# A two-layer YOCO decoder trunk on one core: a second weight unit in the four quarters of the first loads

## The chip, the core and the metric

The kernel runs on one NeuronCore of a Trainium2 chip. The core has five engines with instruction queues of their own: TensorE (PE; PEld is its weight load), VectorE (DVE), ScalarE (ACT), GpSimd (POOL) and SyncE (SP), which here only issues transfers. Each queue is worked off strictly in the order in which it was written; an instruction that has to wait holds up everything behind it on its engine. The metric is the device time of one execution in microseconds (us), lower is better. The kernel before took 583.97 us (median of 3 runs, 583.82 to 584.67).

## The reference

One sequence of 256 tokens with 1024 features passes two layers and a final norm:

```
x = x + short_conv_mixer(rms_norm(x, a_norm), a_w_in, a_conv, a_w_out)     # layer 0
x = x + conv_glu_ffn(rms_norm(x, f_norm[0]), ...)
k, v = shared_kv(x, kv_norm, w_k, w_v)                                     # layer 1
x = x + moba_attention(rms_norm(x, b_norm), w_q, w_o, k, v, rel_bias)
x = x + conv_glu_ffn(rms_norm(x, f_norm[1]), ...)
return rms_norm(x, final_norm)

def rms_norm(x, g):  return x * rsqrt(mean(x * x, axis=-1) + 1e-6) * g
def short_conv_mixer(h, w_in, conv_w, w_out):
    b_gate, c_gate, hx = split(h @ w_in, 3)
    return (b_gate * causal_dwconv(c_gate * hx, conv_w)) @ w_out
```

All is float32. The change lies in the first layer's mixer, in the first 30 us or so.

## The kernel before

**Products.** x is held transposed, as `xT`: 8 tiles of 128 features by 256 tokens. Every float32 product is made of three products of rounded halves (`mm3`, L160): both operands are split into a `hi` part (a copy to a shorter format, by ScalarE, L86) and a `lo` part (what is left, a subtraction by VectorE, L92). TensorE multiplies hi by hi (L161), hi by the input's lo (L162) and the weight's lo by hi (L163). So the third matmul on a weight is the first that needs its `lo`. The norm's factor 1/rms is not applied to x: x is only scaled by the gain (`scaled_hi`, `scaled_lo`), and the products are multiplied by `rr`, the row of factors, when they are read.

**Units.** Weights come in units: "B" of 1 MB (128 x 2048) and "S" of 512 KB (128 x 1024). A unit is loaded by SP (`load`), split (`split_hi`, `split_lo`, also in parts) and then used by matmuls (`up_step`, `down_step`). `hi("B")` and `lo("B")` split the next unit of a kind by counters (`ptr`); a finished `lo` also issues the load of the unit three further on, into the same raw buffer. The mixer has 8 steps: `MC[j]` (B) gives the c gate and the hx part, `MB[j]` (S) the b gate, `MO[j]` (S) is its piece of the output product. A B unit is 48 matmuls, an S unit 24.

**The start.** L134 runs ten float32 matmuls on a tile of ones. `pk`, the table of gains and conv weights, is loaded from ScalarE's queue behind ScalarE's table load. SP loads x, `MC[0]` and `MB[0]` in four quarters (two feature tiles each), then `MC[1]` in four quarters, then whole units. The first loop (L375) takes a quarter of x, `MC[0]` and `MB[0]` at a time. A second loop (L385) splits `MC[1]` in quarters and takes the squares of x (ScalarE), which VectorE sums.

**The factors.** `rstd_cols` (L316) sums the squares over the features with two small matmuls (L320), VectorE makes 1/rms out of it in eleven small steps and two of a diagonal `dg` (L328). `rstd_rows` (L331) turns `dg` into a row with a matmul (L334), which ScalarE copies into `rr`. `mixer_a` (L397) multiplies the products of `MC[j]` by `rr` (L401, L402), and then has in VectorE's queue the `lo` of another unit, the conv taps (L369) and more. `mixer_b` (L413) multiplies by the b gate and splits the result for `MO[j]`. In the order of the program `rstd_cols` stands after six of eight feature tiles of `MC[1]`, `rstd_rows` after two of eight of `MC[2]`. `MB[2]` writes to the bank named `misc`, which `rstd_cols` and `rstd_rows` use as well.

The order on every engine is the order in which the program issues instructions; no scheduler changes it. DMA transfers rotate through eight completion semaphores, so a transfer is issued only when the eighth before it has landed.

Of the kernel before, what the change touches and what calls it, by code (L numbers as in the profile page):

```python
# [32 lines left out]
P_AN, P_KVN, P_BN, P_FN, P_FIN, P_CONV, P_FCW, P_FCB = 0, 8, 16, 24, 40, 48, 72, 336  # L33
# [4 lines left out]
def f32(ap):  # L38
    return ap.bitcast(F32)
# [3 lines left out]
def yoco_kernel(ctx: ExitStack, tc: tile.TileContext, t: dict, out: bass.AP):  # L43
    nc = tc.nc
    V, A, G, PE = nc.vector, nc.scalar, nc.gpsimd, nc.tensor

    const = ctx.enter_context(tc.tile_pool(name="const", bufs=1))
# [12 lines left out]
    ptr = {"B": [0, 0], "S": [0, 0]}  # L60
# [36 lines left out]
    def hi(tag, part=0, parts=1):  # L97

        n = ptr[tag][0]
        if n < len(by_tag[tag]) and (by_tag[tag][n].prev is None or by_tag[tag][n].prev.used):  # L100
            by_tag[tag][n].split_hi(part, parts)
            ptr[tag][0] += part == parts - 1

    def lo(tag, part=0, parts=1):

        n = ptr[tag][1]
        if n < len(by_tag[tag]) and by_tag[tag][n].hi is not None:
            by_tag[tag][n].split_lo(part, parts)
            if part == parts - 1:
                ptr[tag][1] += 1  # L110
                if n + RAW_BUFS[tag] < len(by_tag[tag]):
                    by_tag[tag][n + RAW_BUFS[tag]].load()

    MC = [Unit(t["w_mc"][j], BIG) for j in range(KT)]
    MB, MO = [], []
# [15 lines left out]
    ones = const.tile([128, 128], F32, name="ones")  # L131
    G.memset(ones, 1.0)
    warm = psum.tile([128, 512], F32, name="misc", bufs=1)
    for _ in range(10):  # L134
        PE.matmul(warm[:, :128], ones, ones, start=True, stop=True)
    first = const.tile([128, 1], F32, name="first")
    A.activation(first, ones[:, 0:1], AF.Copy)
    xT = act.tile([128, KT, S], F32, name="xres", bufs=1)
    pk = const.tile([128, P_ALL], F32, name="pk")
    nc.scalar.dma_start(pk[:, :P_FCW], t["pk"][:, :P_FCW])  # L140
    for q in range(4):
        nc.sync.dma_start(xT[:, 2 * q:2 * q + 2, :], t["xT"][:, 2 * q:2 * q + 2, :])
# [13 lines left out]
    def par(c, k=0):  # L156
        return pk[:, c + k:c + k + 1]
# [7 lines left out]
    def up_step(u, o, xh, xl, m, ks=range(KT), first=0, again=False):  # L165

        assert u.lo is not None
        wh, wl = u.v(u.hi, m), u.v(u.lo, m)
        for k in ks:
            h, lw = (xh.again, xl.again) if again and k == 0 else (xh[:, k, :], xl[:, k, :])  # L170
            for i in range(m):
                mm3(o[:, i, :], wh[:, k, i, :], wl[:, k, i, :], h, lw,
                    start=(k == first and i == 0), stop=(k == KT - 1))
        u.used = ks[-1] == KT - 1
# [49 lines left out]
    def acc_bank():  # L224
        return psum.tile([128, 2, S], F32, name="acc", bufs=4)

    def up_bank():
        return psum.tile([128, 2, S], F32, name="up", bufs=3)
# [27 lines left out]
    def parts_tiles(moved=False):  # L256
        return Rows("xh", moved), Rows("xl", moved)
# [17 lines left out]
    def sum_squares(sq, half, order=same):

        f = 4 * half
        V.tensor_add(sq[:, f:f + 2, :], sq[:, f:f + 2, :], sq[:, f + 2:f + 4, :])
        if half:
            V.tensor_add(sq[:, 0:2, :], sq[:, 0:2, :], sq[:, 4:6, :])  # L280
            V.tensor_add(sq[:, 2, :], order(sq[:, 0, :]), order(sq[:, 1, :]))

    def square_tile():
        return act.tile([128, KT, S], F32, name="sq", tag="oh", bufs=1)
# [31 lines left out]
    def rstd_cols(sq):  # L316

        ps = psum.tile([128, 512], F32, name="misc", bufs=1)
        for c in range(2):
            PE.matmul(ps[:, c:c + 1], sq[:, 2, c * 128:(c + 1) * 128], ones[:, 0:1],  # L320
                      start=(c == 0), stop=True, skip_group_check=True)
        w = tmp.tile([128, 8], F32, name="nw")
        ms, y, a = w[:, 0:2], w[:, 2:4], w[:, 4:6]
        V.tensor_scalar(ms, ps[:, 0:2], 1.0 / D, EPS, op0=OP.mult, op1=OP.add)
        rsqrt(ms, y, a)
        dg = tmp.tile([128, 2, 128], F32, name="dg", tag="bias")
        for c in range(2):
            V.tensor_scalar(dg[:, c, :], ident, y[:, c:c + 1], None, op0=OP.mult)  # L328
        return y, dg
# [41 lines left out]

    mc, mb, z = {}, {}, {}
    xh, xl = parts_tiles()
    mc[0], mb[0] = up_bank(), acc_bank()
    for q in range(4):  # L375
        scaled_hi(xT, P_AN, (2 * q, 2 * q + 1), xh)
        scaled_lo(xT, P_AN, (2 * q, 2 * q + 1), xh, xl)
        hi("B", q, 4)
        lo("B", q, 4)
        hi("S", q, 4)  # L380
        lo("S", q, 4)
        up_step(MC[0], mc[0], xh, xl, 2, (2 * q, 2 * q + 1))
        up_step(MB[0], mb[0], xh, xl, 1, (2 * q, 2 * q + 1))
    sq = square_tile()
    for q in range(4):  # L385
        hi("B", q, 4)
        squares(xT, sq, q)
        lo("B", q, 4)
        if q == 2:
            sum_squares(sq, 0)  # L390
    sum_squares(sq, 1)
    tile_0_again(xh, xl)
    hi("S")
# [25 lines left out]
            lo(fill)  # L419
        zl()  # L420

    mc[1] = acc_bank()
    up_step(MC[1], mc[1], xh, xl, 2, range(1, 7), first=1)
    _, dg = rstd_cols(sq)
    for q in range(4):
        hi("B", q, 4)
        lo("B", q, 4)
    hi("S")
    hi("B")
    up_step(MC[1], mc[1], xh, xl, 2, (0, 7), first=1, again=True)  # L430
    mb[1] = acc_bank()
    up_step(MB[1], mb[1], xh, xl, 1)
    mc[2] = up_bank()
    up_step(MC[2], mc[2], xh, xl, 2, range(0, 2))
    rr = rstd_rows(dg)
    A.activation(rr[:, 1, :], rr[:, 0, :], AF.Square)
    lo("S")
    up_step(MC[2], mc[2], xh, xl, 2, range(2, 8))
    mb[2] = psum.tile([128, 512], F32, name="misc", bufs=1).rearrange("p (a s) -> p a s", s=S)
    up_step(MB[2], mb[2], xh, xl, 1)  # L440
    for i in range(2):
# [34 lines left out]
    xh, xl, sq = boundary(acc, xT, P_FN)  # L476
# [85 lines left out]
    xvh, xvl, sq = boundary(acc, xT, P_KVN, rev)  # L562
# [157 lines left out]
    for kind, n in heads:  # L720
        if kind == "v":
            vb[n] = acc_bank() if n < 3 else up_bank()
            if n == 1:
                v_step(1, range(0, 4))
                bias_table(hot)
                ycol, dg = rstd_cols(sq)
# [58 lines left out]
    xh, xl, sq = boundary(acc, xT, P_FN + KT, moved=True)  # L785
# [131 lines left out]
```

## Time and profile before

| | |
|---|---|
| median of 3 runs | 583.97 us |
| the profiled execution | 584.08 us, span 582.1 us |
| TensorE busy | 573.4 us, 98% of the span |
| VectorE busy | 460.9 us, 79% |
| ScalarE busy | 359.7 us, 62% |
| chain that ended last | TensorE 97%, DMA 1%, ScalarE 1% |
| moved | 108.51 MB, 186 GB/s on average |

The span is the time from the first to the last instruction of the program, and lies within the execution's time. Busy shares are averages over the whole program; the chain that ended last is followed back from the last instruction to what released it each time, so its shares say what set the end. With TensorE at 98%, what remains is where it isn't busy, and that is in the first 10 us and at the end.

### The profile page before, as it was taken

How to read it: one execution, taken by the hardware profiler on the slowest of the kernel's cores; microseconds unless marked ns; L12 is line 12 of the kernel's file. 1: busy time of each engine (PE TensorE's matmuls, PEld its weight loads, DVE VectorE, ACT ScalarE, POOL GpSimd, SP SyncE). 2: the span in 40 equal slices, each digit the busy share in tenths (PEclk: the TensorE clock that was granted, in tenths of full speed). 3: DMA queues.
4: the chain of work that ended last, by engine and by line, in shares of the span. 5: the costliest groups of instructions: out<-in, count | busy, mean ns of one | idle time of the engine just before them, and what ended most of it. 6: DMA issues, size and time to landing. Idle time of an engine off the chain costs nothing.

```text
span 582.1 us, 11537 instructions
## 1 busy us (share of the span) xinstructions
PE 573.4 (98%) x4745; PEld 558.4 (96%) x4745; DVE 460.9 (79%) x781; ACT 359.7 (62%) x570; POOL 3.6 (1%) x15
## 2 busy tenths in 40 slices
PE   8999999999999999999999999999999999999995
PEld 8999999999999999999999999999999999999994
DVE  5899769888778777877977887757997787777865
ACT  7765347566566555665758997748675566556443
POOL 0000000000000000000000000000000000000001
PEclk9999999999999999999999999999999999999999
DMA  8985673545554566544446564434655644553111
GB/s 290 404 285 195 214 256 114 212 147 217 217 187 166 191 217 213 173 167 175 147 171 220 181 243 165 145 110 146 218 180 218 216 169 169 207 216 117 65 37 73
DMA packets 24236, 108.51 MB, mean 186 GB/s; under 512 B 2759, under 2 KB 5496, under 8 KB 16248
## 3 DMA queue, kind: packets, MB, share of 16 engines
q1 hardware_dynamic: 23864, 107.46, 52.1%
q8 instruction: 37, 0.61, 0.4%
q10 hardware_dynamic: 320, 0.32, 0.2%
q14 instruction: 15, 0.12, 0.1%
HBM read 106.70 MB, written 1.07 MB: 185 GB/s over the span
## 4 chain that ended last, share of the span: by engine, by line
PE 97%; DMA 1%; ACT 1%; DVE 0%; issue 0%; SPq 0%; POOLq 0%; POOL 0%; DVEq 0%; ACTq 0%
PE up L161 20%; PE up L163 20%; PE up L162 20%; PE acc L161 7%; PE acc L163 7%; PE acc L162 6%; PE acc L189 3%; PE acc L188 3%; PE acc L187 3%; PE acc L623 1%; PE acc L579 1%; PE acc L581 1%; PE acc L582 1%; DMA xres<-xT 1%; PE up L582 0%; PE up L579 0%
## 5 line engine op out<-in xcount | busy, mean ns | idle before, releaser
L161 PE MATMUL up<-xh,hiB 128*128 128x256 f32 x944 | 263.2, 279 | 0.3 <-ACT hiB L86 0.3
L163 PE MATMUL up<-xh,loB 128*128 128x256 f32 x944 | 261.5, 277 | 0.2 <-DVE loB L92 0.2
L162 PE MATMUL up<-xl,hiB 128*128 128x256 f32 x944 | 261.7, 277 | 0.0
L161 PEld LDWEIGHTS up<-xh,hiB 128*128 128x128 f32 x944 | 177.5, 188 | 1.6 <-ACT hiB L86 0.6
L162 PEld LDWEIGHTS up<-xl,hiB 128*128 128x128 f32 x944 | 177.5, 188 | 0.8
L163 PEld LDWEIGHTS up<-xh,loB 128*128 128x128 f32 x944 | 177.4, 188 | 0.7 <-DVE loB L92 0.7
L92 DVE TENSOR_TENSOR loB<-rawB,hiB 128x2048 fp32r<-128x2048 f32 (+2 forms) x75 | 147.6, 1973 | 3.9 <-ACT hiB L86 3.9
L86 ACT ACTIVATE hiB<-rawB 128x2048 fp32r<-128x2048 f32 (+1 forms) x73 | 123.6, 1697 | 17.2 <-PE acc L582 6.0
L92 DVE TENSOR_TENSOR loS<-rawS,hiS 128x1024 fp32r<-128x1024 f32 (+2 forms) x73 | 83.7, 1148 | 13.8 <-ACT hiS L86 13.5
L498 ACT ACTIVATE cv<-u,pk 128x256 f32<-128x256 f32 x88 | 48.2, 595 | 72.8 <-DVE u L491 72.8
L369 DVE SCALAR_TENSOR_TENSOR cv<-u,pk,cv 128x255 f32<-128x255 f32 x192 | 81.4, 479 | 2.7 <-ACT cv L498 1.7
L86 ACT ACTIVATE hiS<-rawS 128x1024 fp32r<-128x1024 f32 (+1 forms) x71 | 71.6, 1010 | 9.7 <-PE acc L162 6.0
L491 DVE TENSOR_TENSOR u<-up,rr 128x512 f32<-128x512 f32 x44 | 30.3, 689 | 58.7 <-PE up L163 57.3
L161 PE MATMUL acc<-sh,hiS 128*128 128x256 f32 x240 | 66.3, 276 | 0.0
L163 PE MATMUL acc<-sh,loS 128*128 128x256 f32 x240 | 66.3, 276 | 0.0
L162 PE MATMUL acc<-sl,hiS 128*128 128x256 f32 x240 | 66.3, 276 | 0.0
L366 ACT ACTIVATE sh<-hid 128x256 fp32r<-128x256 f32 x52 | 21.7, 416 | 59.7 <-DVE hid L512 55.0
L163 PEld LDWEIGHTS acc<-sh,loS 128*128 128x128 f32 x240 | 45.1, 188 | 0.0
L161 PEld LDWEIGHTS acc<-sh,hiS 128*128 128x128 f32 x240 | 45.1, 188 | 0.0
L162 PEld LDWEIGHTS acc<-sl,hiS 128*128 128x128 f32 x240 | 45.1, 188 | 0.0
L189 PE MATMUL acc<-hiS,sl 128*128 128x512 f32 (+1 forms) x89 | 34.8, 391 | 0.0
L188 PE MATMUL acc<-loS,sh 128*128 128x512 f32 (+1 forms) x89 | 34.6, 389 | 0.0
(157 smaller groups left out, 756.9 us busy)
## 6 DMA issues: line engine op xcount, KB each, us to landing
rawB<-w_up SPq DMA_DIRECT2D x44, 1024.0 KB, 4.8
rawS<-w_dn SPq DMA_DIRECT2D x44, 512.0 KB, 3.4
rawB<-w_qk SPq DMA_DIRECT2D x8, 1024.0 KB, 4.9
rawB<-w_mc SPq DMA_DIRECT2D x6, 1024.0 KB, 7.7
rawS<-w_mo SPq DMA_DIRECT2D x8, 512.0 KB, 3.3
rawB<-w_v SPq DMA_DIRECT2D x4, 1024.0 KB, 4.8
rawS<-w_o SPq DMA_DIRECT2D x8, 512.0 KB, 3.5
rawS<-w_mb SPq DMA_DIRECT2D x7, 512.0 KB, 5.6
```

Source lines behind the costliest of these rows:

```text
L86: A.activation(self.hi[:, c], self.raw[:, c], AF.Copy)
L92: V.tensor_sub(self.lo[:, c], self.raw[:, c], f32(self.hi[:, c]))
L161: PE.matmul(o, wh, xh, start=start, stop=False, skip_group_check=True)
L162: PE.matmul(o, wh, xl, start=False, stop=False, skip_group_check=True)
L163: PE.matmul(o, wl, xh, start=False, stop=stop, skip_group_check=True)
L187: PE.matmul(o, hh[:, tok], u.hi[:, f], start=first, stop=False, skip_group_check=True)
L188: PE.matmul(o, hh[:, tok], u.lo[:, f], start=False, stop=False, skip_group_check=True)
L189: PE.matmul(o, hl[:, tok], u.hi[:, f], start=False, stop=last, skip_group_check=True)
L366: return (h, lw), lambda: A.activation(h, src, AF.Copy), lambda: V.tensor_sub(lw, src, f32(h))
L369: V.scalar_tensor_tensor(o[:, back:], u[:, :S - back], w, o[:, back:], op0=OP.mult, op1=OP.add)
L491: V.tensor_mul(u, ub[j], rr[:, 0:1, :].to_broadcast([128, 2, S]))
L498: A.activation(o[:, half, :], u[:, half, :], AF.Identity, scale=cw[half][2], bias=par(P_FCB, c0 + half * FJ))
```

## The change

- The load order: the four quarters of `MC[1]` move into the first loop of loads, each behind the quarter of `MB[0]`. In ScalarE's queue `pk` is issued before the first activation (which loads the activation table), and no longer behind it.
- The warm-up has 7 matmuls instead of 10.
- The first compute loop takes `MC[1]` in with each quarter: 30 matmuls per quarter instead of 18. In its first quarter, x and `MC[0]` are scaled, split and multiplied one feature tile at a time. The squares of a quarter are taken one quarter later, in the same loop; the second loop is gone.
- The counters are set past units 0 and 1, and the loads of `MC[3]` and `MC[4]` are issued behind the loop (before, the `lo` of units 0 and 1 did that).
- `MC[2]` is split before `MB[1]` is multiplied. `rstd_cols` moves from `MC[1]` to `MC[2]`, after three of its eight feature tiles; `rstd_rows` moves to the end of `MC[2]`.

The number of matmuls outside the warm-up stays the same.

```diff
@@ -131,18 +131,17 @@
     ones = const.tile([128, 128], F32, name="ones")
     G.memset(ones, 1.0)
     warm = psum.tile([128, 512], F32, name="misc", bufs=1)
-    for _ in range(10):
+    for _ in range(7):
         PE.matmul(warm[:, :128], ones, ones, start=True, stop=True)
-    first = const.tile([128, 1], F32, name="first")
-    A.activation(first, ones[:, 0:1], AF.Copy)
     xT = act.tile([128, KT, S], F32, name="xres", bufs=1)
     pk = const.tile([128, P_ALL], F32, name="pk")
     nc.scalar.dma_start(pk[:, :P_FCW], t["pk"][:, :P_FCW])
+    first = const.tile([128, 1], F32, name="first")
+    A.activation(first, ones[:, 0:1], AF.Copy)
     for q in range(4):
         nc.sync.dma_start(xT[:, 2 * q:2 * q + 2, :], t["xT"][:, 2 * q:2 * q + 2, :])
         MC[0].load(q, 4)
         MB[0].load(q, 4)
-    for q in range(4):
         MC[1].load(q, 4)
     MB[1].load()
     MC[2].load()
@@ -371,23 +370,30 @@
 
     mc, mb, z = {}, {}, {}
     xh, xl = parts_tiles()
-    mc[0], mb[0] = up_bank(), acc_bank()
+    mc[0], mb[0], mc[1] = up_bank(), acc_bank(), acc_bank()
+    sq = square_tile()
     for q in range(4):
-        scaled_hi(xT, P_AN, (2 * q, 2 * q + 1), xh)
-        scaled_lo(xT, P_AN, (2 * q, 2 * q + 1), xh, xl)
-        hi("B", q, 4)
-        lo("B", q, 4)
+        two = (2 * q, 2 * q + 1)
+        for ks in [(k,) for k in two] if q == 0 else [two]:
+            scaled_hi(xT, P_AN, ks, xh)
+            MC[0].split_hi(ks[0] // len(ks), KT // len(ks))
+            scaled_lo(xT, P_AN, ks, xh, xl)
+            MC[0].split_lo(ks[0] // len(ks), KT // len(ks))
+            up_step(MC[0], mc[0], xh, xl, 2, ks)
         hi("S", q, 4)
         lo("S", q, 4)
-        up_step(MC[0], mc[0], xh, xl, 2, (2 * q, 2 * q + 1))
-        up_step(MB[0], mb[0], xh, xl, 1, (2 * q, 2 * q + 1))
-    sq = square_tile()
-    for q in range(4):
-        hi("B", q, 4)
-        squares(xT, sq, q)
-        lo("B", q, 4)
+        up_step(MB[0], mb[0], xh, xl, 1, two)
+        MC[1].split_hi(q, 4)
+        MC[1].split_lo(q, 4)
+        up_step(MC[1], mc[1], xh, xl, 2, two)
+        if q:
+            squares(xT, sq, q - 1)
         if q == 2:
             sum_squares(sq, 0)
+    ptr["B"] = [2, 2]
+    for u in MC[3:5]:
+        u.load()
+    squares(xT, sq, 3)
     sum_squares(sq, 1)
     tile_0_again(xh, xl)
     hi("S")
@@ -419,23 +425,20 @@
             lo(fill)
         zl()
 
-    mc[1] = acc_bank()
-    up_step(MC[1], mc[1], xh, xl, 2, range(1, 7), first=1)
-    _, dg = rstd_cols(sq)
     for q in range(4):
         hi("B", q, 4)
         lo("B", q, 4)
-    hi("S")
-    hi("B")
-    up_step(MC[1], mc[1], xh, xl, 2, (0, 7), first=1, again=True)
     mb[1] = acc_bank()
     up_step(MB[1], mb[1], xh, xl, 1)
     mc[2] = up_bank()
-    up_step(MC[2], mc[2], xh, xl, 2, range(0, 2))
+    up_step(MC[2], mc[2], xh, xl, 2, range(1, 4), first=1)
+    _, dg = rstd_cols(sq)
+    hi("S")
+    hi("B")
+    up_step(MC[2], mc[2], xh, xl, 2, (0, 4, 5, 6, 7), first=1, again=True)
     rr = rstd_rows(dg)
     A.activation(rr[:, 1, :], rr[:, 0, :], AF.Square)
     lo("S")
-    up_step(MC[2], mc[2], xh, xl, 2, range(2, 8))
     mb[2] = psum.tile([128, 512], F32, name="misc", bufs=1).rearrange("p (a s) -> p a s", s=S)
     up_step(MB[2], mb[2], xh, xl, 1)
     for i in range(2):
```

Lines of the changed kernel differ by one from L138 on, and by more from L373 on: L160 to L162 are the three products there, L319 and L333 the matmuls of the factors, L336 and L440 ScalarE's two steps to `rr`, L407 and L408 the first two steps of `mixer_a`.

SP's queue at the start, before; `xres` is x, `w_mc` and `w_mb` the weights of `MC` and `MB`, and what stands in brackets are the completion semaphores that are waited for:

```order
1 L142 DMA xres<-xT 128x512
2 L80 DMA rawB<-w_mc 128x512
3 L80 DMA rawS<-w_mb 128x256
4 L142 DMA xres<-xT 128x512
5 L80 DMA rawB<-w_mc 128x512
6 L80 DMA rawS<-w_mb 128x256
...
13 L80 DMA rawB<-w_mc 128x512 [waits DMAHW5_49]
...
17 L80 DMA rawS<-w_mb 128x1024 [waits DMAHW1_49]
18 L80 DMA rawB<-w_mc 128x2048 [waits DMAHW2_49]
...
20 L151 DMA pk<-pk 128x352 [waits DMAHW4_49]
21 L80 DMA rawB<-w_mc 128x2048 [waits DMAHW5_49,DVE_49]
22 L80 DMA rawS<-w_mb 128x1024 [waits DMAHW6_49,DVE_49]
```

`MC[1]` had its quarters behind all of x. The same place after:

```order
1 L142 DMA xres<-xT 128x512
2 L80 DMA rawB<-w_mc 128x512
3 L80 DMA rawS<-w_mb 128x256
4 L80 DMA rawB<-w_mc 128x512
5 L142 DMA xres<-xT 128x512
6 L80 DMA rawB<-w_mc 128x512
...
8 L80 DMA rawB<-w_mc 128x512 [waits DMAHW0_49]
...
17 L80 DMA rawS<-w_mb 128x1024 [waits DMAHW1_49]
18 L80 DMA rawB<-w_mc 128x2048 [waits DMAHW2_49]
...
20 L150 DMA pk<-pk 128x352 [waits DMAHW4_49]
21 L80 DMA rawS<-w_mb 128x1024 [waits DMAHW7_49,DMAHW5_49,DVE_49]
22 L80 DMA rawB<-w_mc 128x2048 [waits DMAHW6_49]
```

A quarter of `MC[1]` (128x512) now stands before each further quarter of x, and the load of `MC[3]` (row 22) behind that of `MB[3]` (row 21).

TensorE's queue from the matmul on `dg` to the first matmuls of `MC[3]` (`hiB_339`), before; `hiB_325` is `MC[2]`, `hiS_337` is `MB[2]`:

```order
160 L163 MATMUL up<-xh,loB_327 128x256
161 L334 MATMUL misc<-dg,ones 128x256 [waits PE_49]
162 L161 MATMUL up<-xh,hiB_325 128x256 [waits Activation_49]
...
198 L161 MATMUL misc<-xh,hiS_337 128x256 [waits Activation_49]
199 L162 MATMUL misc<-xl,hiS_337 128x256
200 L163 MATMUL misc<-xh,loS_396 128x256 [waits DVE_49]
...
222 L161 MATMUL up<-xh,hiB_339 128x256
223 L162 MATMUL up<-xl,hiB_339 128x256
224 L163 MATMUL up<-xh,loB_468 128x256 [waits DVE_49]
```

The matmul on `dg` stands in the middle of `MC[2]`. The same after; `hiB_318` is `MC[2]`, `hiS_392` is `MB[2]`, `hiB_394` is `MC[3]`:

```order
165 L319 MATMUL misc<-ones,sq 128x1 [waits PE_49]
...
196 L162 MATMUL up<-xh,loB_320 128x256
197 L333 MATMUL misc<-dg,ones 128x256 [waits DVE_49,PE_49]
198 L160 MATMUL misc<-xh,hiS_392 128x256 [waits Activation_49]
199 L161 MATMUL misc<-xl,hiS_392 128x256
200 L162 MATMUL misc<-xh,loS_431 128x256 [waits DVE_49]
...
222 L160 MATMUL up<-xh,hiB_394 128x256
223 L161 MATMUL up<-xl,hiB_394 128x256
224 L162 MATMUL up<-xh,loB_467 128x256 [waits DVE_49]
```

Between the matmul on `dg` and `MC[3]` stood 60 matmuls (rows 162 to 221), and now 24 (rows 198 to 221).

VectorE's queue from `dg` to the `lo` of `MC[3]` (`loB_468`), before; `loB_327` is that of `MC[2]`, `loS_396` that of `MB[2]`:

```order
27 L324 TENSOR_SCALAR nw<-misc 128x2 [waits PE_49]
28 L305 TENSOR_SCALAR nw<-nw 128x2 [waits DVE_49]
...
38 L328 TENSOR_SCALAR dg<-ident,nw 128x128 [waits DVE_49,Pool_49]
...
40 L92 TENSOR_TENSOR loB_327<-rawB,hiB_325 128x512 [waits DMAHW2_49,Activation_49]
...
42 L92 TENSOR_TENSOR loS_396<-rawS,hiS_337 128x1024 [waits DMAHW3_49,Activation_49]
43 L401 TENSOR_TENSOR u<-up,rr 128x256 [waits Activation_49]
44 L402 TENSOR_TENSOR u<-up,u 128x256 [waits DVE_49]
45 L92 TENSOR_TENSOR loB_468<-rawB,hiB_339 128x2048 [waits DMAHW5_49]
```

The `lo` of `MC[2]` stands behind `dg`. After; `loB_320` is `MC[2]`, `loS_431` is `MB[2]`, `loB_467` is `MC[3]`:

```order
28 L92 TENSOR_TENSOR loB_320<-rawB,hiB_318 128x512 [waits DMAHW2_49,Activation_49]
...
30 L323 TENSOR_SCALAR nw<-misc 128x2 [waits PE_49]
31 L304 TENSOR_SCALAR nw<-nw 128x2 [waits DVE_49]
...
41 L327 TENSOR_SCALAR dg<-ident,nw 128x128 [waits DVE_49,Pool_49]
...
43 L92 TENSOR_TENSOR loS_431<-rawS,hiS_392 128x1024 [waits DMAHW3_49,Activation_49]
44 L407 TENSOR_TENSOR u<-up,rr 128x256 [waits Activation_49]
45 L408 TENSOR_TENSOR u<-up,u 128x256 [waits DVE_49]
46 L92 TENSOR_TENSOR loB_467<-rawB,hiB_394 128x2048 [waits DMAHW6_49]
```

The `lo` of `MC[2]` now stands ahead of the steps that make 1/rms; the `lo` of `MC[3]` stays behind the two steps that read `rr`.

## Rows read from the trace of the kernel before

**Rows 1.** Timeline of TensorE; start us, length us, engine, line, operation [idle before it].

```profile
0.97 4.63 PE L135 MATMUL misc<-ones 128*128 128x128 f32 x20 [0.97 <-POOL ones L132]
5.51 0.58 PE L161 MATMUL up<-xh,hiB 128*128 128x256 f32 x1
...
6.23 0.39 PE L163 MATMUL up<-xh,loB 128*128 128x256 f32 x1
...
8.05 0.28 PE L163 MATMUL acc<-xh,loS 128*128 128x256 f32 x1
...
9.32 0.39 PE L163 MATMUL up<-xh,loB 128*128 128x256 f32 x1 [0.23 <-DVE loB L92]
```

**Rows 2.** The chain that ended last; start us, us, what.

```profile
2.08 5.00 DMA xres<-xT
...
396.41 1.75 PE acc L801 x16
```

**Rows 3.** Timeline of ScalarE and VectorE, first 7 us.

```profile
4.03 0.91 ACT L265 ACTIVATE xh<-xres,pk 128x256 fp32r<-128x256 f32 x2 [1.81 <-DMA pk<-pk]
...
4.84 0.61 ACT L86 ACTIVATE hiB<-rawB 128x512 fp32r<-128x512 f32 x1
...
5.36 0.40 ACT L86 ACTIVATE hiS<-rawS 128x256 fp32r<-128x256 f32 x1
5.49 0.69 DVE L92 TENSOR_TENSOR loB<-rawB,hiB 128x512 fp32r<-128x512 f32 x1
...
6.10 0.42 DVE L92 TENSOR_TENSOR loS<-rawS,hiS 128x256 fp32r<-128x256 f32 x1
```

**Rows 4.** Timeline of TensorE, 19 to 33 us.

```profile
19.42 0.50 PE L320 MATMUL misc<-ones,sq 128*128 128x1 f32 x4
...
21.26 0.28 PE L161 MATMUL acc<-xh,hiS 128*128 128x256 f32 x1
...
23.98 0.28 PE L161 MATMUL up<-xh,hiB 128*128 128x256 f32 x1
...
25.34 0.59 PE L334 MATMUL misc<-dg,ones 128*128 128x256 f32 x2
...
32.83 0.28 PE L163 MATMUL up<-xh,loB 128*128 128x256 f32 x1
```

**Rows 5.** Busy time in a stretch; stretch, length, engines (count), PEclk, DMA, GB/s.

```profile
30.00:40.00 10.00, 10.00 (x91) 10.00 (x90) 9.65 (x17) 6.09 (x8) 0.00 (x0) 1.00 0.84 278
```

**Rows 6.** Timeline of the transfers' issue, first 2 us.

```profile
0.96 0.38 ACTq L140 DMA_DIRECT2D pk<-pk  x1
...
1.15 0.42 SPq L80 DMA_DIRECT2D rawB<-w_mc  x1
```

**Rows 7.** The tile rawB in the first 40 us, its landing times.

```profile
DMA to landing us min/median/max: 3.4/4.9/10.3
```

**Rows 8.** Busy time and transfer rate by microsecond.

```profile
3.00:4.00 1.00, 1.00 (x7) 1.00 (x6) 0.00 (x0) 0.00 (x0) 0.00 (x0) 1.00 0.99 311
4.00:5.00 1.00, 1.00 (x7) 1.00 (x7) 0.43 (x2) 0.97 (x3) 0.00 (x0) 1.00 1.06 299
8.00:9.00 1.00, 0.74 (x5) 0.43 (x4) 0.96 (x3) 1.00 (x4) 0.00 (x0) 1.00 1.04 392
```

**Rows 9.** Timeline of ScalarE and VectorE, from the row of factors on.

```profile
25.98 0.38 ACT L337 ACTIVATE rr<-misc 128x256 f32<-128x256 f32 x1 [0.90 <-PE misc L334]
...
26.84 0.43 DVE L401 TENSOR_TENSOR u<-up,rr 128x256 f32<-128x256 f32 x1 [0.62 <-ACT rr L436]
...
27.64 2.28 DVE L92 TENSOR_TENSOR loB<-rawB,hiB 128x2048 fp32r<-128x2048 f32 x1
```

**Rows 10.** Timeline of VectorE, two places further on.

```profile
49.06 1.22 DVE L92 TENSOR_TENSOR loS<-rawS,hiS 128x1024 fp32r<-128x1024 f32 x1
...
62.72 0.42 DVE L401 TENSOR_TENSOR u<-up,rr 128x256 f32<-128x256 f32 x1 [2.59 <-PE up L163]
```

**Rows 11.** Timeline of TensorE, the first matmuls of MB[4].

```profile
51.87 0.28 PE L163 MATMUL up<-xh,loS 128*128 128x256 f32 x1
```

## The prediction

> **What bounds the kernel now.** I read the share of each engine first: TensorE is busy 98% of the span, and the chain of waits is 97% TensorE. So a change counts only where TensorE waits. The waits by engine, asked for the first 120 us, name TensorE only before 9.4 us. There the timeline shows it [rows 1]: 20 warm-up passes to about 5.5 us, a first real matmul at 5.51, the first one on a `lo` half at 6.23, the 18th and last of the first quarter at 8.05, and then nothing steady until 9.32. The chain of waits names the cause: the second quarter of x, issued at 2.08, took 5.00 us to land [rows 2]. ScalarE's start is held by `pk`, not by x [rows 3]. From 9.32 on TensorE issues a 256-column matmul every 0.1134 us (24 of `MB[1]` from 21.26 to 23.98 [rows 4]).
>
> The second thing to read is what runs just ahead of being needed. From 30 to 40 us VectorE is busy 9.65 of 10 us [rows 5]: its queue has hardly a gap, and everything in it from the unit-0 mixer on waits for `rr`, which comes out of the L334 matmul at 25.34.
>
> **The front, a gain.** The change must be followed to the same amount of work: 120 matmuls (48 of `MC[0]`, 24 of `MB[0]`, 48 of `MC[1]`). Before, two stood before 6.23 and the rest ended at 21.26 [rows 4]: 15.03 us for 118 matmuls, 13.38 at 0.1134, plus the L320 group that lies among them (0.50) [rows 4]. So about 1.1 us of waiting is in there, nearly all of it between 8.05 and 9.32.
>
> - Splitting tile by tile: ScalarE copies 128x256 in 0.40 us instead of 128x512 in 0.61, VectorE subtracts in 0.42 instead of 0.69 [rows 3]: 0.21 + 0.27 = 0.48 us off the way to the first `lo` matmul. Only one `xh` stands ahead of the copy and `pk` comes up to 0.24 us sooner (issued at 0.96 in ScalarE's queue [rows 6], now first); the copy cannot start before its weights: issued at 1.15, landed 3.4 us later at the earliest [rows 7], some 4.6 instead of 4.84. So the first `lo` matmul comes near 5.5, 0.7 earlier. Two more instructions on each engine (0.19 and 0.15 us) fit before q1.
> - Thirty matmuls per quarter instead of 18 take 3.40 us instead of 2.04 and cover more of the wait. But 256 KB more stand before each later x. In the old order the transfer that ended at byte 896 KB landed at 7.08 [rows 2]; in the new one that byte ends the first quarter of `MC[1]`. Its copy (0.6) and subtraction (0.7) [rows 3] make the third matmul on it ready at 8.4, where TensorE is there at about 7.8: 0.65 us of wait. The second quarter of x comes 256 KB later, 0.67 us at 392 GB/s [rows 8], near 7.75; 0.91 for its two `xh`, 0.55 for the copy (0.61 with overlap) and 0.7 for the subtraction bring its `lo` to 9.95, with TensorE there at 9.75: 0.2. From there ScalarE needs about 2.8 us per quarter (two `xh` 0.91, copies 0.61, 0.40 and 0.61, squares as long as a copy, less some overlap) and VectorE 2.7, under TensorE's 3.40, so squares and the second unit's split are hidden.
>
> Gain: 0.7 + 1.1 - 0.85 = 0.95 us. Bounds: 1.8 if no load is late; 0.3 if the loads are 0.65 us later still.
>
> **The rstd chain, a loss.** Sums, squares and the two L320/L334 groups are as many as before and cost the same; they are moved. Before, L334 stood with 36 matmuls of `MC[2]` and 24 of `MB[2]` behind it before `MC[3]` began. Now it stands behind all of `MC[2]`: 36 x 0.1134 = 4.08 us of cover gone. In this chain nothing is new, so each price is in the trace: L334 at 25.34, ScalarE reads it at 25.98, VectorE's L401 starts at 26.84, L402 behind it, and then, in the same queue, the `lo` half of `MC[3]`: 27.64 plus 2.28 [rows 9]. TensorE follows a `lo` by 0.05 (5.49 + 0.69 against 6.23 [rows 1, 3]). From L334 to the third matmul of `MC[3]` that is 4.63 us. TensorE used to arrive there at 32.83 [rows 4], 7.49 after L334; now 7.49 - 4.08 = 3.41 after. Wait: 1.22 us. (Part of it is taken sooner: `MB[2]` writes the bank that L334 wrote, so its first matmul waits until `rr` is read, 0.64 + 0.38 after L334; that lies inside the 4.63.)
>
> It doesn't end there, because VectorE's queue is full. The matmuls of `MB[4]` need a `lo` that ended at 49.06 + 1.22 = 50.28 [rows 10], 1.6 us before TensorE asked for it at 51.87 [rows 11]; that was the smallest lead of this kind up to there. Counted from L334 it is 24.99 us of VectorE's work (50.33 - 25.34), the same after the change, and TensorE arrives 51.87 - 25.34 - 4.08 = 22.45 after: it waits 2.54 us in all, the 1.22 contained in it. Behind it VectorE had 2.59 us of idle before unit 5's mixer [rows 10], so nothing more comes due.
>
> Bounds of this term: 1.22, if VectorE catches up after `MC[3]`; 2.9, if `rr` itself is late by the 0.4 that ScalarE might still be busy with `MC[3]`'s copy (its load now comes behind a 512 KB one). I take 2.54, since it comes from rows of the very instructions that run.
>
> **The sum.** 2.54 - 0.95 = +1.6 us. The profiled execution took 584.08 us (span 582.1 and 2.0 around it), 0.1 above the median of the three runs, 583.97. So 585.7 against the profile, 585.6 against the median. The move of the table load behind the `pk` issue costs nothing: ScalarE idled 1.81 us there [rows 3].
>
> **The warm-up** drops from 20 passes to 14, and ends 6 x 0.21 = 1.3 us earlier, near 4.2. A pass took 0.21 us, while a transpose of the same 128x128 shape later takes 1.75 / 16 = 0.11 [rows 1, 2]: the two differ as TensorE's two levels, 1.2 and 2.4 GHz, do, though the granted clock of these stretches reads 1.00 [rows 8]. In this run TensorE was fast soon after 6.23 (15 matmuls from there to 8.05 in 1.82 us [rows 1]), after unbroken work. Now TensorE idles some 1.0 us between warm-up and first matmul, so the rise may come later. The Trainium skill (TensorE: Matmul & The Clock Gate, Part 1: The HAM clock gate) says that half rate is the default and sustained activity releases it; by that rule a shorter warm-up followed by a gap can only delay the rise. The trace agrees as far as it goes.
>
> **Rivals.**
> 1. The front gains all of it and VectorE catches up: 1.22 - 1.8 = -0.6 at best, +0.3 with the middle gain; about 583.8, no change. For it: VectorE has small gaps (0.35 us in 10 [rows 5]). Against it: they are latencies within its own chain.
> 2. The clock rises late. If 18 matmuls, as many as a first quarter of before, run at the slow level, each costs another 0.114: 2.0 us, of which the 0.85 of waits for loads hides a part: +1.2, together 586.8. For it: the idle after the warm-up; against it: the work up to 4.2 may be enough.
> 3. The loads are late: x of the second quarter at 8.4 instead of 7.75, gain 0.3, total +2.2: 586.2. For it: 299 to 311 GB/s in the microseconds 3 to 5 against 392 later [rows 8].
> 4. `rr` is no bound at all and the gain stands: 584.0 - 0.95 or more, 583.0 to 582.2, faster. Against it: the order on VectorE, where the `lo` of `MC[3]` stands behind L407 and L408, which read `rr`.
>
> **Chances.** Forecast 0.42 (its own range 584.8 to 586.3), rival 1 0.20, rival 2 0.18, rival 3 0.15, rival 4 0.05. Leaving out half of rival 1's low side, rival 4 and the far end of rival 2 gives 583.6 to 587.2. What this kernel's measurement can tell from no change is about 0.2%, 1.17 us: slower means above 585.14. The forecast gives about three quarters of its chance to slower (0.32), rivals 2 and 3 all (0.33); same gets 0.10 and most of rival 1 (0.19); faster rival 4 and a little of rival 1. So 0.06, 0.29, 0.65.
>
> **What would show it.** Right: TensorE's last matmul of `MC[1]` near 19.9 (L320 no longer before it); behind the L333 group a wait of about 0.8 us for ScalarE's `rr`, one of some 0.5 for the `lo` of `MC[3]`, and a further wait or two for VectorE up to `MB[4]`, 2.5 us in all; VectorE's idle before unit 5's mixer shorter than 2.59. Wrong: no TensorE wait between 27 and 55 us (rival 4), only the first two (rival 1); warm-level matmuls 0.23 apart beyond 6.5 us (rival 2); a wait for x of more than 0.5 us at the second quarter (rival 3).

## The result, and the profile after

The changed kernel takes 588.72 us (median of 4 runs, 586.93 to 589.67) against 584.26 us for the kernel before on the same chip: 1.0076 times, 95% interval 1.0062 to 1.0091, some 4.5 us slower. Forecast were 585.6 us and a range up to 587.2: the direction is right, the size is not.

The first lines of the page of the changed kernel's profiled execution (586.93 us), the span and TensorE's busy time:

```profile
span 584.8 us, 11524 instructions
...
PE 573.7 (98%) x4739; PEld 557.9 (95%) x4739; DVE 461.0 (79%) x782; ACT 359.7 (62%) x571; POOL 3.6 (1%) x15
```

TensorE is busy for 573.7 us, 573.4 before, although its warm-up is 1.28 us shorter (3.35 us, before 4.63); the span is 2.7 us longer. So part of the loss in this execution is waiting, and part is work that takes longer, of which more below. The engine's waits in the first 60 us of the same trace (engine, line, what was waited for: us, times, longest):

```profile
PE misc L135 <- POOL ones L132: 1.0, 1, 1.0
PE up L160 <- ACT hiB L86: 1.0, 1, 1.0
PE acc L162 <- DVE loS L92: 0.8, 1, 0.8
PE misc L160 <- ACT rr L336: 0.5, 1, 0.5
PE up L162 <- DVE loB L92: 0.5, 2, 0.2
```

Before, nothing stood in this list after 9.4 us. The places of these waits are in TensorE's timeline of the same trace (start, length, engine, line, operation, idle before), whose rows answer to [rows 1, 4, 11]:

```profile
0.97 3.35 PE L135 MATMUL misc<-ones 128*128 128x128 f32 x14 [0.97 <-POOL ones L132]
5.30 0.39 PE L160 MATMUL up<-xh,hiB 128*128 128x256 f32 x1 [0.97 <-ACT hiB L86]
...
5.76 0.39 PE L162 MATMUL up<-xh,loB 128*128 128x256 f32 x1
...
9.06 0.28 PE L162 MATMUL acc<-xh,loB 128*128 128x256 f32 x1
9.46 0.38 PE L160 MATMUL up<-xh,hiB 128*128 128x256 f32 x1
9.68 0.28 PE L161 MATMUL up<-xl,hiB 128*128 128x256 f32 x1
10.18 0.39 PE L162 MATMUL up<-xh,loB 128*128 128x256 f32 x1 [0.23 <-DVE loB L92]
...
20.53 0.28 PE L162 MATMUL acc<-xh,loB 128*128 128x256 f32 x1
...
29.51 0.59 PE L333 MATMUL misc<-dg,ones 128*128 128x256 f32 x2
30.57 0.39 PE L160 MATMUL misc<-xh,hiS 128*128 128x256 f32 x1 [0.47 <-ACT rr L336]
...
43.39 0.38 PE L162 MATMUL acc<-sh,loS 128*128 128x256 f32 x1 [0.81 <-DVE loS L92]
...
54.41 0.39 PE L162 MATMUL up<-xh,loS 128*128 128x256 f32 x1
```

In these rows a matmul that had to wait is known by its length: 0.38 or 0.39 us in place of 0.28, and the next one starts 0.22 us behind it. The first `lo` matmul is only 0.47 us earlier than before. The last matmul of `MC[1]` starts at 20.53, where the forecast had it near 19.9, and the next unit at 20.65 (before 21.26, with the 0.50 us of the L320 group inside). `MB[4]` is reached at 54.41, 2.54 us later than in [rows 11]. The forecast had 2.54 - 0.95 = 1.59 us there; that the chain's 2.54 comes back in this difference is chance. ScalarE's first step on x's second quarter, in the same trace:

```profile
7.97 0.91 ACT L264 ACTIVATE xh<-xres,pk 128x256 fp32r<-128x256 f32 x2 [1.19 <-DMA xres<-xT]
```

It waits for the load, and TensorE stands 0.67 us longer than its step at that quarter's first three matmuls (9.46 and 10.18).

VectorE's timeline of the same trace from `rr` on answers to [rows 9, 10]:

```profile
31.00 0.42 DVE L407 TENSOR_TENSOR u<-up,rr 128x256 f32<-128x256 f32 x1 [0.60 <-ACT rr L440]
31.46 0.42 DVE L408 TENSOR_TENSOR u<-up,u 128x256 f32<-128x256 f32 x1
31.80 2.28 DVE L92 TENSOR_TENSOR loB<-rawB,hiB 128x2048 fp32r<-128x2048 f32 x1
...
65.38 0.42 DVE L407 TENSOR_TENSOR u<-up,rr 128x256 f32<-128x256 f32 x1 [1.18 <-PE up L162]
```

From L333 at 29.51 to L407 it is 1.49 us (1.50 before), to the end of that `lo` 4.57; VectorE's idle before unit 5's mixer has shrunk from 2.59 to 1.18 us.

### The profile page after: what moved, and what is told of

Same layout as the page of the kernel before. It is cut to its first block, busy times and chain, and to the rows that moved or that the text cites. A ratio compares the mean times of both kernels' runs of the same rounds, so it can differ in the third digit from the quotient of the medians.

```text
span 584.8 us, 11524 instructions
## 1 busy us (share of the span) xinstructions
PE 573.7 (98%) x4739; PEld 557.9 (95%) x4739; DVE 461.0 (79%) x782; ACT 359.7 (62%) x571; POOL 3.6 (1%) x15
## 4 chain that ended last, share of the span: by engine, by line
PE 94%; DVE 2%; DMA 1%; ACT 1%; issue 0%; SPq 0%; POOLq 0%; POOL 0%; DVEq 0%; ACTq 0%
PE up L160 20%; PE up L161 19%; PE up L162 19%; PE acc L162 6%; PE acc L161 6%; PE acc L160 6%; PE acc L188 3%; PE acc L187 3%; PE acc L186 3%; PE acc L626 1%; PE acc L582 1%; PE acc L585 1%; PE acc L584 1%; DMA xres<-xT 1%; DVE loB L92 1%; DVE loS L92 0%
## 5 line engine op out<-in xcount | busy, mean ns | idle before, releaser
L160 PE MATMUL up<-xh,hiB 128*128 128x256 f32 x944 | 263.0, 279 | 1.1 <-ACT hiB L86 1.0
L162 PE MATMUL up<-xh,loB 128*128 128x256 f32 x944 | 261.8, 277 | 0.5 <-DVE loB L92 0.5
L160 PEld LDWEIGHTS up<-xh,hiB 128*128 128x128 f32 x944 | 177.4, 188 | 2.5 <-ACT hiB L86 1.6
L162 PEld LDWEIGHTS up<-xh,loB 128*128 128x128 f32 x944 | 177.4, 188 | 1.0 <-DVE loB L92 1.0
L92 DVE TENSOR_TENSOR loB<-rawB,hiB 128x2048 fp32r<-128x2048 f32 (+3 forms) x76 | 147.6, 1947 | 3.4 <-ACT hiB L86 3.3
L86 ACT ACTIVATE hiB<-rawB 128x2048 fp32r<-128x2048 f32 (+2 forms) x74 | 123.7, 1676 | 18.9 <-PE acc L585 6.0
L162 PE MATMUL acc<-sh,loS 128*128 128x256 f32 x240 | 66.4, 277 | 0.8 <-DVE loS L92 0.8
L160 PE MATMUL acc<-sh,hiS 128*128 128x256 f32 x240 | 66.3, 276 | 0.0
L162 PEld LDWEIGHTS acc<-sh,loS 128*128 128x128 f32 x240 | 45.0, 188 | 1.0 <-DVE loS L92 1.0
L160 PEld LDWEIGHTS acc<-sh,hiS 128*128 128x128 f32 x240 | 45.1, 188 | 0.0
```

The source lines that it names most:

```text
L86: A.activation(self.hi[:, c], self.raw[:, c], AF.Copy)
L92: V.tensor_sub(self.lo[:, c], self.raw[:, c], f32(self.hi[:, c]))
L160: PE.matmul(o, wh, xh, start=start, stop=False, skip_group_check=True)
L162: PE.matmul(o, wl, xh, start=False, stop=stop, skip_group_check=True)
```

## The experiments

Two theories first: A, the loss is the rstd chain; B, the shorter warm-up costs clock. Theory D came up with the first traces: TensorE's step from matmul to matmul isn't constant.

**The warm-up back.**

```diff
-    for _ in range(7):
+    for _ in range(10):
```

> The changed kernel with the ten warm-up matmuls of before. Theory A (the loss is the rstd chain, 2.5 us, and nothing else but small things): as the changed kernel, 588.7, within 0.5. Theory B (TensorE spends part of its first matmuls at the lower clock level because the warm-up is shorter and an idle gap follows): 586.5 to 587.3, near the changed kernel's fastest run (586.9), and the spread of its runs shrinks from 2.7 us to about 1.

588.54 us, 1.0073 of before (1.006 to 1.0086). Taken by the median, B falls. That reading was too quick: the six times are 586.35, 586.42 and four from 588.35 to 589.0, so two groups, and a median of six from such a mixture says little.

**The kernel before with the shorter warm-up.**

```diff
-    for _ in range(10):
+    for _ in range(7):
```

> The kernel before with seven warm-up matmuls instead of ten, nothing else changed. Theory A: no change, 584.3 within 0.4. Theory B: slower by 1 to 2 us, 585.3 to 586.3, with a wider spread of its runs.

585.04 us, 1.0014 (1.0005 to 1.0022): the warm-up costs 0.9 us there. TensorE's timeline of this kernel shows how:

```profile
5.20 0.58 PE L161 MATMUL up<-xh,hiB 128*128 128x256 f32 x1 [0.87 <-ACT hiB L86]
...
9.30 0.41 PE L163 MATMUL acc<-xh,loS 128*128 128x256 f32 x1
9.51 0.41 PE L161 MATMUL up<-xh,hiB 128*128 128x256 f32 x1
9.72 0.39 PE L162 MATMUL up<-xl,hiB 128*128 128x256 f32 x1
9.94 0.29 PE L163 MATMUL up<-xh,loB 128*128 128x256 f32 x1
10.06 0.28 PE L161 MATMUL up<-xh,hiB 128*128 128x256 f32 x1
```

Up to 9.7 us the matmuls are 0.21 us apart, from 9.94 on 0.12: the lower of the two levels, 1.2 GHz, and then the upper. The clock is not all of it in this execution. L334 comes at 26.26, 0.92 us later than before. At the first `lo` of the second quarter it is 0.62 (9.94 against 9.32 in [rows 1]); the other 0.30 is a step of 0.118 us in place of 0.113 from there to about 21 us.

**The kernel before with the late chain alone.** `rstd_cols`, with the two splits behind it, and `rstd_rows` go to the places of the changed kernel; loads, loops and warm-up stay.

```diff
-    _, dg = rstd_cols(sq)
+    up_step(MC[1], mc[1], xh, xl, 2, (0, 7), first=1, again=True)
...
-    up_step(MC[2], mc[2], xh, xl, 2, range(0, 2))
+    up_step(MC[2], mc[2], xh, xl, 2, range(0, 3))
+    _, dg = rstd_cols(sq)
+    hi("S")
+    hi("B")
+    up_step(MC[2], mc[2], xh, xl, 2, range(3, 8))
     rr = rstd_rows(dg)
```

> The kernel before with the two steps to the row of factors where the change has them: the column sums after three tiles of MC[2], the row at the end of MC[2]. Loads, loops and warm-up stay. Theory A: slower by 2.5 us, 586.8; TensorE waits for rr behind the matmul on dg (0.8 us), for the lo of MC[3] (0.5), for the lo of MO[0] (about 1) and a little at MB[4]. Theory B: no change, 584.3 within 0.5.

586.71 us, 1.0055 (1.0039 to 1.0072); the lower three times are 586.15 to 586.28, the upper three, which have no trace, 587.14 to 589.23. The timeline of the lowest has the waits of the changed kernel, at the same distances:

```profile
28.73 0.60 PE L334 MATMUL misc<-dg,ones 128*128 128x256 f32 x2
29.80 0.39 PE L161 MATMUL misc<-xh,hiS 128*128 128x256 f32 x1 [0.47 <-ACT rr L337]
...
42.62 0.39 PE L163 MATMUL acc<-sh,loS 128*128 128x256 f32 x1 [0.81 <-DVE loS L92]
...
53.65 0.39 PE L163 MATMUL up<-xh,loS 128*128 128x256 f32 x1
```

**The changed kernel with the chain early.** `rstd_cols` goes ahead of `MB[1]`, `rstd_rows` behind three tiles of `MC[2]`.

```diff
+    _, dg = rstd_cols(sq)
+    hi("S")
+    hi("B")
     mb[1] = acc_bank()
...
     up_step(MC[2], mc[2], xh, xl, 2, range(1, 4), first=1)
-    _, dg = rstd_cols(sq)
-    hi("S")
-    hi("B")
-    up_step(MC[2], mc[2], xh, xl, 2, (0, 4, 5, 6, 7), first=1, again=True)
     rr = rstd_rows(dg)
     A.activation(rr[:, 1, :], rr[:, 0, :], AF.Square)
     lo("S")
+    up_step(MC[2], mc[2], xh, xl, 2, (0, 4, 5, 6, 7), first=1, again=True)
```

> The changed kernel with the column sums before MB[1] and the row of factors after three of eight tiles of MC[2], so that 54 matmuls stand between the matmul on dg and MC[3] (60 before, 24 in the change). Warm-up of seven as in the change. Theory A: faster than the changed kernel by 2.5 us, 586.2, and no wait of TensorE between 25 and 60 us. Theory B alone: 588.7, as the changed kernel. If both hold, 586.2 with the changed kernel's spread of 2.7 us.

585.02 us, 1.0023 (1.0011 to 1.0036), 3.7 us under the changed kernel. The waits between 27 and 60 us are gone. One is new that the expectation didn't have: in the trace L333 itself waits 0.3 us for `dg`, up to 26.38. Ten of twelve times lie from 584.10 to 585.25, two at 587.72 and 588.41; the one at 587.72 is the profiled one, and its matmuls stand 0.1178 us apart from 21 to 106 us, 0.1133 from 11 to 20 us.

**Both undone,** e4 with ten warm-up matmuls:

> The changed kernel with two edits: ten warm-up matmuls in place of seven, and rstd_cols of unit 2 ahead of MB[1] with rstd_rows after three tiles of MC[2], as in e4_early_rstd. If the warm-up is worth the 0.9 us that separated e2_before_warm7 from the kernel before (585.04 against 584.11), this is 585.0 less 0.9 = 584.1, the kernel before's time, and the front of the change is worth nothing. If the shorter warm-up costs the changed kernel nothing, as e1_warm10 let one think (588.54 against 588.72), this stays at 585.0. If the front gains the 0.95 of the prediction once the chain is away, it is 583.2.

583.96 us, 1.0003 (0.9994 to 1.0012): the warm-up is worth 1.06 us here, and this is the time of the kernel before (584.14 on the same chip). With the two losses out, the front gains nothing that the times can tell from none: the interval leaves room for 0.35 us, not for 0.95. In the trace L333 is 0.41 us earlier (25.61 instead of 26.02, which is 25.34 plus the six matmuls that now stand ahead of it). TensorE's waits over the first 60 us of this kernel, all that this list has:

```profile
PE misc L135 <- POOL ones L132: 1.0, 1, 1.0
PE up L162 <- DVE loB L92: 0.2, 1, 0.2
```

**The front alone in the kernel before:** tile by tile in the first quarter, and `pk` first.

```diff
+        if q == 0:
+            for k in two:
+                scaled_hi(xT, P_AN, (k,), xh)
+                MC[0].split_hi(k, KT)
+                scaled_lo(xT, P_AN, (k,), xh, xl)
+                MC[0].split_lo(k, KT)
+                up_step(MC[0], mc[0], xh, xl, 2, (k,))
```

> The kernel before with the front edits alone: the first quarter split tile by tile, and the parameters ahead of the rest in their queue; loads, warm-up and the chain of unit 2 as before. The prediction's term for the front was 0.95 us, of which the first lo matmul is 0.7: if that holds, 583.2. If the first matmuls of the third quarter, which wait for x q1, take back what the front gives (the wait for it ended at 7.08 in the kernel before), no change, 584.1.

584.33 us, 1.0007 (0.9998 to 1.0016): no gain. The first `lo` matmul is at 5.70 instead of 6.23, but the two waits of before at 8.59 and 9.32 come back at 8.09 and 8.81, a third at 11.31 is new, and L334 comes at 25.30, as before (25.34).

**The load order.** On top of e5, x's second quarter goes ahead of the first quarter of `MC[1]`; in f2, `pk` moreover goes behind the table load again.

```diff
+        if q == 1:
+            MC[1].load(0, 4)
         MC[0].load(q, 4)
         MB[0].load(q, 4)
-        MC[1].load(q, 4)
+        if q:
+            MC[1].load(q, 4)
```

> The kernel of e5_early_rstd_warm10 (583.96) with one edit: the second quarter of x is issued ahead of the first quarter of the second unit's weights, 256 KB sooner. In e5_early_rstd_warm10 TensorE waits 0.26 us at 9.39 for xh of that quarter and 0.50 at 10.12 for its lo. If the load order is what eats the front's gain, both go: 583.2. If the wait only moves to the first matmul on the second unit's quarter, which then lands 256 KB later, no change: 584.0.

> As f1_x_q1_sooner, with the parameters issued behind the table load again, as in the kernel before. In three looks at the changed kernel ScalarE's first copy, which waits for the parameters, starts at 4.35, 4.67 and 4.49 us, in two looks at kernels with the old order at 4.03 and 3.72, though the new issue is 0.24 us sooner. If the order is the cause, the first copy starts near 3.9, the first lo matmul 0.4 to 0.5 us sooner than in f1_x_q1_sooner, and the time is up to that much less. If it is chance, both are the same. The prediction had the new order up to 0.24 us sooner, so by it this is slower by that or equal.

585.95 us, 1.0029 (1.0013 to 1.0046), and 585.54, 1.0026 (1.0012 to 1.004). No gain: in f1 the wait goes to `MC[1]`'s own quarter, at 8.06 and 8.79. The times fall apart: six of f1 at 583.84 to 584.56 and six at 587.34 to 587.9, six of f2 at 583.58 to 584.38 and six at 586.69 to 587.54. On `pk` they decide nothing. ScalarE's first copy starts at 4.29 us in f1 and 4.20 in f2; over all traces it is 4.21 to 4.67 (once 5.20) with `pk` first and 3.72 to 4.20 with `pk` second, so issuing it 0.24 us sooner did not make it land sooner.

**The two groups.** The changed kernel four more times, the kernel of e1 three more times, that of f1 once more, each with its trace:

> The changed kernel itself, a second look, to catch the trace of a run near 588.5 us: the profiled run took 586.93, the median is 588.72. Theory D, that a wait of TensorE can leave its 128x256 matmuls at 117.8 ns a step in place of 113.3 until the next wait: a run of 588 us or more shows the longer step from the last wait of the chain, near 54 us, to about 105 us (some 420 matmuls by 4.5 ns, about 2 us), and a run near 587 does not. The rival, that the upper runs lose their 2 us in the middle or at the end of the span: the steps up to 105 us are the same in both.

> The changed kernel itself, a third look with the same purpose as a2_after_again: by theory D its time goes with the number of 128x256 matmuls that are issued 117.8 ns apart, 4.5 ns for each; by the rival the two are unrelated.

> The changed kernel, a fourth look. By the two parts found so far its time follows from the trace: 586.9 with the clock up by about 5 us and the step at 113.3 ns from 56 us on; about 1.2 more if the matmuls up to 10 us are 0.21 us apart; about 2 more if the step is 117.8 ns from 56 to 106 us. A time more than 0.5 us off that sum would mean a third part.

> The changed kernel, a fifth look, expected by the same sum as a4_after_fourth.

> The kernel of e1_warm10, a second look, to catch a run of its upper group (its six times were 586.35, 586.42 and four from 588.35 to 589.0). Theory D: such a run has the full clock from about 5.2 us on and 128x256 matmuls 117.8 ns apart from the chain's last wait near 54 us to about 105 us, 2.2 us in all. The rival: its clock rises only near 10 us, as in a2_after_again and a3_after_third, and the step has no part in it.

> The kernel of e1_warm10, a third look with the same purpose as g1_warm10_again: near 586.4 the step after 54 us is 113.3 ns, near 588.6 it is 117.8 ns to about 105 us; by the rival the step is the same in both and the clock's rise differs.

> The kernel of e1_warm10, a fourth look: 586.2 with the step at 113.3 ns behind the chain's last wait, about 588.4 with 117.8 ns, and the clock up by 7 us in both.

> The kernel of f1_x_q1_sooner, whose twelve times fall into 583.84 to 584.56 and 587.34 to 587.9. The step alone: a run of the upper half has 117.8 ns from about 27 to about 105 us, 78 us / 0.1178 x 4.5 ns = 3.0 us, and no wait that the profiled run at 584.25 doesn't have. Otherwise the upper half has a wait of its own.

| | us | idle before the first product | lower level until | step, 12 to 18 us | `dg` matmul | from there to the end | step, 60 to 100 us |
|---|---|---|---|---|---|---|---|
| before | 584.08 | none | 5.5 | 113 ns | 25.34 | 556.8 | 113 ns |
| after, profiled | 586.93 | 0.97 | not seen | 118 ns | 29.51 | 555.3 | 113 ns |
| a2 | 588.17 | 1.28 | 9.9 | 118 ns | 30.79 | 555.4 | 113 ns |
| a3 | 590.03 | 1.09 | 9.9 | 118 ns | 30.68 | 557.3 | 118 ns |
| a4 | 585.77 | 1.13 | not seen | 113 ns | 28.37 | 555.3 | 113 ns |
| a5 | 586.42 | 0.80 | 8.6 | 113 ns | 29.25 | 555.3 | 113 ns |
| g1 (warm-up 10) | 586.12 | none | 6.4 | 113 ns | 28.81 | 555.4 | 113 ns |
| g2 (warm-up 10) | 585.94 | none | 6.7 | 113 ns | 28.78 | 555.3 | 113 ns |
| g3 (warm-up 10) | 587.59 | 0.55 | 9.6 | 113 ns | 30.32 | 555.4 | 113 ns |
| e1 (warm-up 10) | 586.35 | 0.07 | not seen | 118 ns | 28.96 | 555.4 | 113 ns |
| e2 | 585.15 | 0.87 | 9.5 | 118 ns | 26.26 | 556.8 | 113 ns |
| e3 | 586.15 | 0.63 | not seen | 113 ns | 28.73 | 555.4 | 113 ns |
| e4 | 587.72 | 1.03 | not seen | 113 ns | 26.38 | 559.2 | 118 ns |
| e5 (warm-up 10) | 583.89 | none | 5.8 | 113 ns | 25.61 | 556.1 | 113 ns |
| e6 | 584.22 | 0.14 | not seen | 113 ns | 25.30 | 556.8 | 113 ns |
| f1 | 584.25 | 0.18 | not seen | 113 ns | 25.88 | 556.2 | 113 ns |
| f2 | 583.58 | 0.19 | not seen | 113 ns | 25.23 | 556.2 | 113 ns |
| f3 (as f1) | 587.96 | none | 6.1 | 113 ns | 26.56 | 559.2 | 118 ns |

(Times of the `dg` matmul, L333 or L334, are starts; the lower level is over behind the last product with a record of 0.41 us or more; from there to the end is the span less the start of the `dg` matmul; steps are medians.)

The expected sums missed. a2, at 588.17, does not have the longer step behind 54 us that theory D asked for. a4 and a5 came 1.1 and 1.7 us under their sum, and g3 1.4 us over its own, since its clock was not up by 7 us. The sum of a4 and a5 started from the profiled execution, whose `dg` matmul stands 1.14 us behind a4's: 0.56 are there at the first `lo` of x's second quarter (10.18 against 9.62), by its waits for that quarter, and the rest comes by the longer step from 10 to 27 us. This is the third part that the expectation of a4 speaks of.

Two things make most of the difference from one execution of the changed kernel to the next. The first is the clock. In a3, TensorE's timeline at the start and around its last wait:

```profile
5.42 0.58 PE L160 MATMUL up<-xh,hiB 128*128 128x256 f32 x1 [1.09 <-ACT hiB L86]
...
9.70 0.41 PE L161 MATMUL acc<-xl,hiB 128*128 128x256 f32 x1
9.91 0.41 PE L162 MATMUL acc<-xh,loB 128*128 128x256 f32 x1
10.12 0.31 PE L160 MATMUL acc<-xh,hiB 128*128 128x256 f32 x1
10.28 0.28 PE L161 MATMUL acc<-xl,hiB 128*128 128x256 f32 x1
...
55.12 0.28 PE L161 MATMUL up<-xl,hiB 128*128 128x256 f32 x1
55.23 0.28 PE L162 MATMUL up<-xh,loB 128*128 128x256 f32 x1
55.34 0.28 PE L160 MATMUL up<-xh,hiS 128*128 128x256 f32 x1
55.46 0.28 PE L161 MATMUL up<-xl,hiS 128*128 128x256 f32 x1
55.60 0.38 PE L162 MATMUL up<-xh,loS 128*128 128x256 f32 x1
55.83 0.28 PE L160 MATMUL up<-xh,hiS 128*128 128x256 f32 x1
55.94 0.28 PE L161 MATMUL up<-xl,hiS 128*128 128x256 f32 x1
56.06 0.28 PE L162 MATMUL up<-xh,loS 128*128 128x256 f32 x1
56.18 0.28 PE L160 MATMUL up<-xh,hiS 128*128 128x256 f32 x1
56.30 0.28 PE L161 MATMUL up<-xl,hiS 128*128 128x256 f32 x1
```

Twenty-one matmuls up to 9.9 us are at the lower level, 0.21 us apart. (The granted clock of 5 to 10 us reads 1.00 all the same, in the row below; the spacing tells the level.) The second is the step: up to the wait at 55.60 the matmuls follow each other by 0.11 to 0.12 (0.1133 on average), behind it by 0.1178, with the same shapes and the upper level. The sums over 60 to 100 us show that it stays (stretch, length, TensorE busy and its count of matmuls, granted clock, DMA share, GB/s); of the profiled execution, then of a3 (with its 5 to 10 us), then of f3:

```profile
60.00:100.00 40.00, 40.00 (x356) 1.00 0.63 215
```

```profile
5.00:10.00 5.00, 4.58 (x21) 1.00 1.02 345
60.00:100.00 40.00, 40.00 (x342) 1.00 0.66 227
```

```profile
60.00:100.00 40.00, 40.00 (x342) 1.00 0.60 211
```

From 60 to 100 us TensorE is full in all three, and does 14 matmuls less in two. A count of matmuls, then, finds what the busy share hides. In a3, 50 us / 0.1178 x 4.5 ns = 1.9 us, and "from there to the end" is 557.3 in place of 555.3; in f3 the longer step holds from 21 to 106 us, 3.0 us more of it than in f1, and that column is 559.2 in place of 556.2. So the step makes 3.0 of the 3.7 us between these two executions. The other 0.7 lies ahead of the `dg` matmul, part of it a wait at 13.94 that f1's trace doesn't have, against the expectation. The upper half of f1 has only this one trace. The four upper times of e1 have none; a step as in a3 or f3 would make them (586.2 and 1.9 to 3.0 more, 588.1 to 589.2), but that is argued, not shown.

## Why the prediction was wrong

- **The rstd chain: right, place by place.** `rr` late for `MB[2]` (0.85 us between starts), the `lo` of `MC[3]` (0.5), `MO[0]` (1.1) and `MB[4]`: the wait of some 0.8, the one of 0.5 and "a further wait or two". By the table, 36 matmuls (4.08 us) left the part behind the `dg` matmul, which got only 1.4 to 1.5 shorter: a loss of 2.6 to 2.7 us, forecast 2.54. It is the same in nine traces of three kernels, and e3 has it alone. Rivals 1 and 4 are out: VectorE didn't catch up.
- **The front: 0.95 us was too much.** The forecast puts the `dg` matmul at 25.34 + 4.08 - 0.95 = 28.47. In a4 it is at 28.37, and the execution took 585.77, forecast 585.6. That agreement is luck, for even there the parts are not those of the text: the first `lo` came 0.26 sooner, not 0.7 (the copy waits for `pk`, which landed later, not up to 0.24 sooner), `MC[1]`'s first quarter cost no wait (0.65 forecast), and the second quarter of x little. In the profiled execution the 0.85 us of waits were not far off, but stood in another place: nothing at `MC[1]`'s first quarter, 0.67 at x's second, where the text had 0.2. That quarter was used from 7.97 on (7.75 forecast), and TensorE, not held up before, came sooner. Over all times of e5 no gain shows (at most 0.35 us by the interval). In e6, where `MC[1]` doesn't join the quarters, the front gains nothing.
- **The step that failed is the warm-up's: the sum 2.54 - 0.95 has no term for it.** The text saw the idle time between warm-up and first product, and gave the late rise a chance of 0.18 and 586.8 us. The late rise happens in three of five traces of the changed kernel (a2, a3, a5), and puts the `dg` matmul 0.9 us (a5) to 2.4 us (a2) behind that of a4. Part of that in a2 and a3, some 0.65 us, is the longer step from 10 to 27 us, and a2's first product came 0.14 us later as well. In the other two traces the rise came no later than before: the first product has a record of 0.39 us in the profiled execution (5.30), of 0.58 in [rows 1] (5.51). The Trainium skill (TensorE: Matmul & The Clock Gate, Part 1: The HAM clock gate) has half rate as the default, released by sustained activity; these traces agree (a3: 0.21 us apart to 9.9 us, then 0.12). What the text made of it, that a shorter warm-up "can only delay the rise", is not borne out by those two. That the shorter warm-up costs about 1 us is measured twice by medians, 0.93 (e2) and 1.06 (e5 against e4); how much of it is clock alone only single traces show, 0.62 of 0.92 in e2's.
- **What no step of it had: a pitch that isn't constant.** All terms used 0.1134 us per matmul. The profiled execution ran its first loop at 0.1178 from 10 to 25 us, some 127 matmuls by 4.5 ns, 0.6 us; with the waits for x's second quarter that used up the whole front gain. a3 has the longer step behind the chain's last wait as well, which brings it to 590.03: 584.1 + 2.6 (chain) + 1.3 (`dg` matmul at 30.68 instead of 29.42) + 1.9 = 589.9.
- **The range** took in the clock at 1.2 us but let it stand alone; chain, clock and step add up. Of the 4.5 us between the medians, 2.6 are the chain and about 1 the warm-up, and the front gave next to nothing back. The 0.9 us that remain fit the longer step, which is argued and not shown: the median of 588.72 belongs to executions without a trace.
- **Rival 3** (loads late): its sign, more than 0.5 us of wait at x's second quarter, is there in the profiled execution (0.67), its condition is not: the quarter was there by 7.97, not 8.4. Another load was late in g3: `pk` let ScalarE start at 5.20, TensorE idled even behind ten warm-up matmuls, and the lower level held to 9.6.

No version beats the kernel before: e5 equals it.

## What to carry to other kernels

Moving work ahead of a chain takes away the cover behind it: count, from the instruction that starts the chain, what both engines have to do until they meet again, and look for the smallest lead further on, not only at the first meeting. Before shortening a warm-up, ask how long the engine stands idle between it and the first product, and in how many executions. And where times fall into groups, take traces from each of them before believing a median: here a median of six hid the cost of the warm-up.

## What the runs showed of the hardware

- **Clock.** In nine traces with at least 0.5 us of idle between the warm-up and the first product, the lower level lasted to 8.6 to 9.9 us in five and wasn't seen in four; in nine with 0.2 us or none, it was over by 7 us every time. What decides among the first nine stays open: 0.80 us of idle had it, 1.13 didn't. In five traces with ten warm-up matmuls (e1, e3, e6, f1, f2) the passes ended at 4.98 to 5.49 us instead of 5.61, so there the clock rose within the warm-up, and the idle time behind it decided nothing.
- **Two steps at the upper level.** The same 128x256 matmuls are issued 113.3 or 117.8 ns apart, with records of 276 or 281 ns. The longer step set in behind a wait, at the rise of the clock (a2, a3, e2) or behind the small groups L319 and L333, and once held for 85 us. Which one comes is not fixed by the program: f1 and f3 are the same kernel. But the program bears on how often times of an upper group come: none of the 74 times of the kernel before lies above 585.16, two of twelve of e4 lie above 587, six of twelve of f1. What chooses the step stays open; nothing was tried that selects it.
- **A wait costs more than itself:** at the upper level the matmul behind it takes 0.39 us, and the next starts 0.22 us later instead of 0.11.
